# One sum of squares for both query tiles of a turn, taken after the second tile's projection

## The chip, the cores and the metric

The kernel runs on one core of one Trainium2 chip. The metric is the device time of one execution in microseconds; of several runs the median is compared. Lower is better. Engines are named as in the profile: PE (TensorE), ACT (ScalarE), DVE (VectorE), POOL (GpSimd), SP (SyncE, which issues the DMAs). PSUM is the memory that PE writes and that ACT and DVE read; POOL does not touch it here.

## What is computed

One layer of a hybrid decoder, for a prompt of 2048 tokens and 8 single-token samples, all in fp32. What matters for this change is the query path:

```python
h = _rmsnorm(x, norm_g) * (1.0 + scale) + shift
z = h @ w_in                                    # 1024 -> 6656 columns: q, k, v, gates, ...
q = _rmsnorm(q.reshape(B, T, N_HEADS, HEAD_DIM), q_g)     # 16 heads of 64
k = _rmsnorm(k.reshape(B, T, KV_HEADS, HEAD_DIM), k_g)    # 4 heads of 64
logits = einsum('bnqkgd,bnskd->bnkgqs', qb, kb) * ATT_SCALE + rel_bias   # banded, window 128
p = softmax over [logits, sink]
o = einsum('bnkgqs,bnskd->bnqkgd', p, vb)
ya = o * silu(ga)
```

Each query head is divided by the root of the mean of its 64 squares before the scores. The rest of the layer (a recurrent branch, gates, merge and output projection) is not touched.

## The kernel before

**Halves and turns.** The prompt is done in two halves (s = 0 and 1) of 1024 tokens, eight tiles of 128 tokens each. Each half has a key/value phase, then the attention phase (`phase_attn`), then a long planned stage of large matmuls. The attention phase is a software pipeline of N + 2 = 18 turns of the loop over `i`. `seq` lists 16 steps (u, tp): u is one of four groups of four heads, tp one of four pairs of token tiles. A turn works on three steps at once:

- step i: project the queries of two token tiles (`gemm_a`, 24 matmuls of 128x256 for each tile, both into one PSUM tile `ps_[i]`), square them on ACT and sum each head's 64 squares on DVE (`stage_a1`), turn the sums into reciprocal norms on POOL (`rstd_of`: one multiply-add, then a power of -0.5), and scale the queries on DVE (`stage_a2`);
- step i-1: transpose the scaled queries (`stage_b1`: PE, then ACT and DVE split them in a high and a low part), scores (`stage_b2`, PE), band, bias and row minimum on DVE and exponentials on ACT (`stage_b3`, once for each of the two tiles). The exponential's tile `lt` has a 129th column with the sink, which POOL copies there (`stage_b0`);
- step i-2: reciprocal of the row sums (DVE) and multiplication with it (POOL) (`stage_b4`), transposes of the probabilities (`stage_c1`: PE, then ACT copies them out and DVE multiplies with the causal mask `mcT`), the product with the values (`stage_c2`, PE) and the evacuation (`stage_c3`: on DVE where u is 0, on ACT otherwise).

**Order.** Inside the loop `pinned[0]` is set, so every engine's queue holds its instructions in the order in which the loop's code calls them, but for small moves of the scheduler; waits between engines are semaphores that the framework places by tile. A tile that PE, ACT and DVE share in PSUM is passed from one to the next. On PE a turn is: first tile's 24 projection matmuls, 4 transposes of `stage_b1`, second tile's 24 matmuls, 8 transposes of `stage_c1` (four for each tile, waiting for POOL's product), scores, values, next turn.

**Weights.** In some turns `weights` splits raw weights in two parts (a CAST on ACT, a subtraction on DVE); two such splits stand near the start of a turn.

**Buffers.** `M` tiles hold small statistics, `H` tiles come from a pool of six, `Tt` takes the oldest idle one of 35 numbered buffers ("B" in the profile) and `free` puts it back at the end of the list. In the profile nearly all instructions carry line L60, a helper; they are told apart by their tiles: `H<-pg` on ACT is the square, `M<-H` on DVE the sum of squares, `M<-M,mhalf` on POOL the power, `B<-pg,M` on DVE the scaling, `B<-B,M` 128x129 on ACT the exponential, `B<-B,M` 128x512 on POOL the product of `stage_b4`, `pt<-ident,B` on PE the transposes, `B<-skn` on POOL the copy of the sinks, `maskf` and `mcT` the masks, and `S<-pt` on ACT the evacuation `stage_c3`.

Of the kernel before, what the change touches and what calls it, by code (L numbers as in the profile page):

```python
# [15 lines left out]
AF = mybir.ActivationFunctionType  # L16
ALU = mybir.AluOpType
AX = mybir.AxisListType
# [8 lines left out]
HD = 64  # L27
# [14 lines left out]
def tile_hybrid_step(ctx: ExitStack, tc: tile.TileContext, x_prompt, x_sample, cache_k, cache_v, state_conv,  # L42
# [24 lines left out]
    V, A, G_, T_, ld = (Pinned(e) for e in (nc.vector, nc.scalar, nc.gpsimd, nc.tensor, nc.sync))  # L67
# [14 lines left out]
    def nm(s):  # L82
        cnt[0] += 1
        return f"{s}_{cnt[0]}"
# [14 lines left out]
    S, Tt = (r.get for r in rings)  # L99

    def free(*ts):
        for t in ts:
            r = rings[id(t) in rings[1].held]
            r.idle.append(r.held.pop(id(t))[1])

    def H(shape, dt=F32):
        return hp.tile([P] + shape, dt, tag="H", name=nm("H"))

    def M(shape, dt=F32):

        return mp.tile([P] + shape, dt, tag="M", name=nm("M"))

    def PG():
        return pg.tile([P, 512], F32, tag="g", name=nm("pg"))
# [4 lines left out]
    def PT():  # L119
        return pt.tile([P, 512], F32, tag="t", name=nm("pt"))  # L120
# [30 lines left out]
    def drop(ws):  # L151

        seen = set()
        for w in ws:
            if id(w[2][0]) not in seen:
                seen.add(id(w[2][0]))
                free(*w[2])
# [33 lines left out]
    def gemm_a(ps, wu, xs, c0, h):  # L191

        o = ps[:, h * 256:(h + 1) * 256]
        for k in range(KT):
            wh, wl, _ = wu[k]
            xh, xl = col(xs, k, c0, P)
            T_.matmul(o, xh, wh, start=(h == 0 and k == 0), stop=False, skip_group_check=True)
            T_.matmul(o, xh, wl, start=False, stop=False, skip_group_check=True)
            T_.matmul(o, xl, wh, start=False, stop=(k == KT - 1), skip_group_check=True)
# [40 lines left out]
    def rstd_of(dst, ss, n, inv):  # L240
        G_.tensor_scalar(dst, ss, inv, EPS, op0=ALU.mult, op1=ALU.add)
        G_.tensor_tensor(dst, dst, mhalf[0:dst.shape[0], 0:n], op=ALU.pow)
# [9 lines left out]
    ps = PT()  # L252
# [305 lines left out]
    def phase_attn(s, hT, sa, kT, vt, chunks, line):  # L558

        ya, mbs, kcs = {}, {}, {}  # L560

        def stage_a1(ps, ss, t):
            sq = H([256])
            A.activation(sq, ps[:, t * 256:(t + 1) * 256], AF.Square)
            o = ss[:, 4 * t:4 * t + 4]
            V.tensor_reduce(o, sq.rearrange("p (h d) -> p h d", d=HD), op=ALU.add, axis=AX.X)
            rstd_of(o, o, 4, 1.0 / HD)

        def stage_a2(ps, ss):
            qn = Tt([2, 2, 2, HD])  # L570
# [73 lines left out]
        def stage_b4(lt, sm):  # L644
            V.reciprocal(sm, sm)
            G_.tensor_tensor(lt[:, :, 0:P], lt[:, :, 0:P], sm.unsqueeze(2).broadcast_to([P, 4, P]), op=ALU.mult)
            return lt
# [69 lines left out]
        N = len(seq)  # L717
# [14 lines left out]
        def ga_half(n):  # L732


            f, c, h = GA[n // nt], n % nt // 2, n % 2
            c0, w = chunks[c]
            if h == 0:
                gps[0] = PG()
                if c == 0 and f < KT:
                    ya[f] = S([1024])  # L740
            ps = gps[0]
            for k in range(4 * h, 4 * h + 4):
                wh, wl, _ = wga[f][k]
                xh, xl = col(hT, k, c0, w)
                T_.matmul(ps[:, :w], wh, xh, start=(k == 0), stop=False)
                T_.matmul(ps[:, :w], wh, xl, start=False, stop=False)
                T_.matmul(ps[:, :w], wl, xh, start=False, stop=(k == KT - 1))
            if h == 0:
                return None

            def evac_ma():
                t = Tt([512])
                A.activation(t[:, :w], ps[:, :w], AF.Tanh, scale=0.5)
                st.dma_start(tmad[s, f - KT, :, c0:c0 + w], t)
                free(t)

            def evac():
                sg = ya[f]
                t = Tt([512])
                A.activation(t[:, :w], ps[:, :w], AF.Tanh, scale=0.5)  # L760
                V.scalar_tensor_tensor(sg[:, c0:c0 + w], t[:, :w], 1.0, ps[:, :w], op0=ALU.add, op1=ALU.mult)
                free(t)

            if c == len(chunks) - 1:
                drop(wga.pop(f))
            return evac if f < KT else evac_ma
# [46 lines left out]
        ps_, ss_, qn_, qk_, c_, sm_, lt_ = {}, {}, {}, {}, {}, {}, {}  # L813
        for i in range(N + 2):
            gsm_ready = len(gsm)

            def fill(n):
                nonlocal hdone
                while hdone < n:
                    evac = ga_half(hdone)  # L820
                    if evac:
                        evac()
                    hdone += 1

            def slot(n):
                if N - 3 <= i <= N:
                    line.emit(4 * (i - N - 1) + n)

            if 2 <= i:
                lt_[i - 2] = [stage_b4(*sm_[i - 2][0])]  # L830
            weights(2 * i, 0)
            if 2 <= i:
                lt_[i - 2].append(stage_b4(*sm_.pop(i - 2)[1]))
            if 1 <= i <= N:
                ub, tb = seq[i - 1]
                if tb == 0 and ub % 2 == 0:
                    mbs[ub // 2] = S([8, P])
                    ld.dma_start(mbs[ub // 2], Md[:, ub // 2 * 8:ub // 2 * 8 + 8])
            slot(0)
            if i < N:  # L840
                u, tp = seq[i]
                ps_[i], ss_[i] = PG(), M([8])
                gemm_a(ps_[i], wqs[u], hT, 2 * tp * P, 0)
                stage_a1(ps_[i], ss_[i], 0)
            elif i == N:
                fill(nh - 3)
            else:
                line.emit(0)
            if 1 <= i <= N:
                qk_[i - 1] = stage_b1(ub, tb, qn_.pop(i - 1))  # L850
            weights(2 * i, 1)
            slot(1)
            if i < N:
                if s == 1 and tp == 1:
                    next(smp[u])
                if pend:
                    next(pend.pop(0))
                gemm_a(ps_[i], wqs[u], hT, (2 * tp + 1) * P, 1)
                if pend:
                    next(pend.pop(0))  # L860
                if tp == 3:
                    drop(wqs.pop(u))
                if s == 1 and tp == 1:
                    next(smp[u])
                stage_a1(ps_[i], ss_[i], 1)
            elif i == N:
                fill(nh - 2)
            else:
                line.emit(1)
            weights(2 * i + 1, 0)  # L870
            if 2 <= i:
                t2 = seq[i - 2][1]
                c_[i - 2] = [stage_c1(2 * t2 + t, lt) for t, lt in enumerate(lt_.pop(i - 2))]
                c_[i - 2] = [fn() for fn in c_[i - 2]]
            slot(2)
            if i == N + 1:
                line.emit(2)
            if 1 <= i <= N:
                lps = stage_b2(ub, tb, *qk_.pop(i - 1))
                lts = [stage_b0(ub) for _ in range(2)]  # L880
            if 2 <= i:
                u2, t2 = seq[i - 2]
                po = stage_c2(u2, c_.pop(i - 2))
                if u2 == 3:
                    free(vt[1][t2])
            if 1 <= i <= N:
                sm_[i - 1] = [stage_b3(ub, 2 * tb, lps[0], lts[0])]
            if i < N:
                qn_[i] = stage_a2(ps_.pop(i), ss_.pop(i))
            if 2 <= i and u2 > 0:  # L890
                stage_c3(u2, t2, po)
            if 1 <= i <= N:
                sm_[i - 1].append(stage_b3(ub, 2 * tb + 1, lps[1], lts[1]))
                if ub % 2 and tb == 3:
                    free(mbs.pop(ub // 2), *kT[ub // 2])
            fill(want[i] if i < N else nh)
            if 2 <= i and u2 == 0:
                stage_c3(u2, t2, po)
            if 2 <= i and t2 == 3:
                for f in (2 * u2, 2 * u2 + 1):  # L900
                    st.dma_start(yad[s, f], ya[f])
                    free(ya.pop(f))
            weights(2 * i + 1, 1)
            if s == 1 and i < N and tp > 0:
                next(smp[u])
            if gsm and gsm_ready:
                next(gsm.pop(0))
            slot(3)
# [1108 lines left out]
    for f in range(KT):  # L2017
# [19 lines left out]
        for tt in range(4):  # L2037
            c = slice(tt * P, (tt + 1) * P)
            for j in range(2):
                wh, wl, _ = wkv[f // 4][j][f % 4]  # L2040
                o = kvp[tt][:, j * 256:(j + 1) * 256]
# [51 lines left out]
    ps = PT()  # L2093
# [51 lines left out]
```

## Time and profile before

| what | value |
|---|---|
| median of 3 runs | 1988.05 us (1987.31 to 1990.62) |
| profiled execution | 1991.77 us, span 1990.1 us, clock 0.995 |
| busy: PE / PE weight loads / DVE / ACT / POOL | 1930.7 / 1571.9 / 1375.0 / 988.4 / 409.4 us |
| attention phase, steady turns | first half about 152 to 316 us of the span, second about 1092 to 1266 us |
| a steady turn | 11 to 13 us |

A row of the timeline gives start, length, engine, operation with the tiles it writes and reads, and, in brackets, how long the engine had stood idle before it and for whom. PE is 97% busy, so the share of busy time says little of what one change is worth; the few idle moments of PE and what ends them say more.

### The profile page before, as it was taken

To read this page: it belongs to the slowest core of one execution; us is meant where nothing else is said; L and a number is where in the kernel's file an instruction comes from. 1 tells how busy PE (TensorE), PEld (TensorE's weight loads), DVE (VectorE), ACT (ScalarE), POOL (GpSimd) and SP (SyncE) were. 2 spreads that over 40 slices of the span, in tenths; PEclk is the share of its full clock that TensorE was granted. 3 is DMA by queue.
4 is the path that set the end of the run, shared out by engine and by line. 5 is a ranking of instruction groups with operands and counts; after the bars stand their busy time and mean duration, and the time that the engine had idled before them with its cause. 6 is when DMAs were issued, how large, how long until landed. Compare 5 with 4: busy or idle time off the path is not lost. (4 is left out here: it accounts for less than half of the span.)

```text
span 1990.1 us, 32504 instructions
## 1 busy us (share of the span) xinstructions
PE 1930.7 (97%) x11504; PEld 1571.9 (79%) x11504; DVE 1375.0 (69%) x2894; ACT 988.4 (50%) x2199; POOL 409.4 (21%) x540
## 2 busy tenths in 40 slices
PE   6899999999999999999999999999999999999999
PEld 4788887778888878887898888777887877777777
DVE  3447777766878885578744766677677879754965
ACT  4335555435665766514423555543465757542221
POOL 4113443000201112152012344310011111111600
PEclk9999999999999999999999999999999999999999
DMA  9520214552433457986622121445233334458673
GB/s 304 178 75 12 86 49 148 151 183 87 150 98 113 143 180 226 321 296 191 224 60 57 36 62 49 143 130 153 78 118 100 127 102 164 141 174 291 219 230 111
DMA packets 307688, 286.62 MB, mean 144 GB/s; under 512 B 57073, under 2 KB 224229, under 8 KB 307486
## 3 DMA queue, kind: packets, MB, share of 16 engines
q1 hardware_dynamic: 307398, 282.41, 45.3%
q8 instruction: 90, 1.47, 0.3%
q0 software_dynamic: 128, 2.15, 0.3%
q14 instruction: 72, 0.59, 0.1%
HBM read 200.69 MB, written 85.93 MB: 144 GB/s over the span
## 5 line engine op out<-in xcount | busy, mean ns | idle before, releaser
L60 PE MATMUL pg<-S,B 128*128 128x512 f32 (+1 forms) x4224 | 1003.8, 392 | 4.2 <-DVE B L60 3.8
L60 PEld LDWEIGHTS pg<-S,B 128*128 128x128 f32 (+1 forms) x4224 | 773.5, 188 | 189.5 <-issue 11.9
L60 DVE TENSOR_TENSOR B<-B,B 128x512 fp32r<-128x512 f32 (+1 forms) x732 | 537.8, 757 | 157.7 <-ACT B L60 147.9
L60 PE MATMUL pq<-S,B 128*128 128x512 f32 (+2 forms) x1920 | 411.0, 378 | 5.9 <-DVE B L60 5.7
L60 PEld LDWEIGHTS pq<-S,B 128*128 128x128 f32 (+1 forms) x1920 | 316.3, 187 | 84.1 <-DVE B L60 9.7
L60 POOL TENSOR_TENSOR B<-B,B 128x512 f32<-128x512 f32 x128 | 191.3, 1511 | 926.3 <-DVE B L60 518.3
L60 ACT CAST B<-B 128x512 fp32r<-128x512 f32 x468 | 280.3, 617 | 111.2 <-DVE B L60 72.1
L60 PE MATMUL pg<-B,S 128*128 128x256 f32 x1872 | 249.0, 289 | 17.6 <-ACT H L60 12.8
L60 PEld LDWEIGHTS pg<-B,S 128*128 128x128 f32 x1872 | 231.9, 192 | 36.6 <-ACT H L60 19.8
L60 ACT CAST S<-B 128x512 fp32r<-128x512 f32 x184 | 108.8, 620 | 95.8 <-DVE B L60 40.3
L60 DVE TENSOR_TENSOR S<-B,S 128x512 fp32r<-128x512 f32 x184 | 143.2, 808 | 14.8 <-ACT S L60 14.6
L60 ACT ACTIVATE B<-B 128x512 f32<-128x512 f32 (+1 forms) x150 | 93.1, 630 | 116.4 <-DVE B L60 108.7
L60 ACT ACTIVATE B<-B,M 128x129 f32<-128x129 f32 x260 | 102.6, 396 | 72.1 <-DVE M L60 53.4
L60 POOL TENSOR_TENSOR B<-B,M 128x512 f32<-128x512 f32 x64 | 70.4, 1121 | 170.4 <-DVE M L60 170.4
L60 DVE SCALAR_TENSOR_TENSOR B<-B,pg 128x512 f32<-128x512 f32 x78 | 53.1, 682 | 74.8 <-PE pg L60 67.0
L60 POOL TENSOR_TENSOR M<-M,mhalf 128x4 f32<-128x4 f32 (+3 forms) x102 | 96.3, 944 | 8.5
L60 DVE TENSOR_TENSOR B<-pq,B 128x512 f32<-128x512 f32 x96 | 65.9, 686 | 44.1 <-PE pq L60 37.9
L60 ACT COPY B<-pg 128x512 f32<-128x512 f32 x80 | 46.9, 586 | 90.1 <-PE pg L60 81.7
L60 DVE TENSOR_REDUCE M<-H 128x4 f32<-128x256 f32 (+1 forms) x85 | 35.1, 414 | 80.3 <-ACT H L60 79.0
L60 ACT COPY H<-pt 128x256 f32<-128x256 f32 (+1 forms) x47 | 15.6, 333 | 150.1 <-PE pt L60 150.1
L60 DVE SCALAR_TENSOR_TENSOR B<-B,VT,B 128x512 f32<-128x512 f32 x96 | 81.1, 845 | 2.3
L60 DVE SCALAR_TENSOR_TENSOR B<-B,B 128x512 f32<-128x512 f32 x106 | 72.0, 684 | 0.4 <-ACT B L60 0.2
(201 smaller groups left out, 1711.5 us busy)
## 6 DMA issues: line engine op xcount, KB each, us to landing
B<-in_w_in_dram SPq DMA_DIRECT2D x144, 256.0 KB
B<-in_w_in_dram SPq DMA_DIRECT2D x128, 128.0 KB
B<-yad SPq DMA_DIRECT2D x56, 256.0 KB
B<-hd SPq DMA_DIRECT2D x48, 256.0 KB
B<-in_w_out_dram SPq DMA_DIRECT2D x48, 256.0 KB
S<-in_w_ada_dram SPq DMA_DIRECT2D x32, 256.0 KB
S<-in_x_prompt_dram SPq DMA_DIRECT2D x16, 512.0 KB
hd<-B SPq DMA_DIRECT2D x32, 256.0 KB
```

The lines of the kernel that those rows point to most:

```text
L60: ins = fn(*args, **kw)
```

## The change

The square and the sum of squares are no longer taken tile by tile. Before, each tile's 256 columns were squared right after that tile's 24 matmuls, summed by head into four columns, and turned into four reciprocal norms. Now ACT squares all 512 columns of the PSUM tile once, after the second tile's matmuls (`stage_a1`, into a B buffer instead of an H tile), and DVE sums all eight heads at once and POOL takes all eight reciprocal norms at once in a new `stage_a3`, which is called later: after `stage_c1`'s mask multiplications and ahead of the scores.

```diff
-        def stage_a1(ps, ss, t):
-            sq = H([256])
-            A.activation(sq, ps[:, t * 256:(t + 1) * 256], AF.Square)
-            o = ss[:, 4 * t:4 * t + 4]
-            V.tensor_reduce(o, sq.rearrange("p (h d) -> p h d", d=HD), op=ALU.add, axis=AX.X)
-            rstd_of(o, o, 4, 1.0 / HD)
+        def stage_a1(ps):
+            sq = Tt([512])
+            A.activation(sq, ps, AF.Square)
+            return sq
+
+        def stage_a3(sq):
+            ss = M([8])
+            V.tensor_reduce(ss, sq.rearrange("p (h d) -> p h d", d=HD), op=ALU.add, axis=AX.X)
+            free(sq)
+            rstd_of(ss, ss, 8, 1.0 / HD)
+            return ss
...
                 gemm_a(ps_[i], wqs[u], hT, 2 * tp * P, 0)
-                stage_a1(ps_[i], ss_[i], 0)
...
                 gemm_a(ps_[i], wqs[u], hT, (2 * tp + 1) * P, 1)
...
-                stage_a1(ps_[i], ss_[i], 1)
+                sq = stage_a1(ps_[i])
...
                 c_[i - 2] = [fn() for fn in c_[i - 2]]
+            if i < N:
+                ss_[i] = stage_a3(sq)
             slot(2)
```

What this does to the queues is shown for one turn of the first half (i = 7; the buffer numbers differ between the kernels).

DVE, from a weight split and the two reciprocals of `stage_b4` to the first mask of the scores, before:

```order
L60 TENSOR_TENSOR B_2583<-B_1962,B_2582 128x512
L60 RECIPROCAL M_2558<-M_2558 128x4
L60 RECIPROCAL M_2577<-M_2577 128x4
L60 TENSOR_REDUCE M_2591<-H_2616 128x4
L60 SCALAR_TENSOR_TENSOR B_2627<-pt_2621,qg_944,B_2626 128x512
L60 TENSOR_TENSOR B_2631<-B_1965,B_2630 128x512
L60 TENSOR_REDUCE M_2591<-H_2664 128x4
L60 TENSOR_TENSOR B_2679<-pt_2669,mcT_90 128x512
L60 TENSOR_TENSOR B_2683<-pt_2674,mcT_90 128x512
L60 COPY_PREDICATED pq_2687<-maskf_88,pq_2687 128x2x128
```

and with the change:

```order
L60 TENSOR_TENSOR B_2548<-B_1941,B_2547 128x512
L60 RECIPROCAL M_2523<-M_2523 128x4
L60 RECIPROCAL M_2542<-M_2542 128x4
L60 SCALAR_TENSOR_TENSOR B_2586<-pt_2580,qg_944,B_2585 128x512
L60 TENSOR_TENSOR B_2590<-B_1944,B_2589 128x512
L60 TENSOR_TENSOR B_2635<-pt_2625,mcT_90 128x512
L60 TENSOR_TENSOR B_2639<-pt_2630,mcT_90 128x512
L60 TENSOR_REDUCE M_2643<-B_2623 128x8
L60 COPY_PREDICATED pq_2647<-maskf_88,pq_2647 128x2x128
```

Two sums of four heads, one before the query split and one ahead of the mask multiplications, have become one sum of eight heads between the mask multiplications (`mcT`) and the scores' first mask (`maskf`).

PE in the same turn, with the semaphores waited for: the four transposes of `stage_b1` between the two tiles' projections, before:

```order
L60 MATMUL pt_2621<-ident_81,B_2563 128x128 [waits DVE_49,PE_49]
L60 MATMUL pt_2621<-ident_81,B_2563 128x128
L60 MATMUL pt_2621<-ident_81,B_2563 128x128 [waits DVE_49]
L60 MATMUL pt_2621<-ident_81,B_2563 128x128
L60 MATMUL pg_2590<-B_1711,S_337 128x256 [waits Activation_49]
```

and with the change:

```order
L60 MATMUL pt_2580<-ident_81,B_2528 128x128 [waits DVE_49,PE_49]
L60 MATMUL pt_2580<-ident_81,B_2528 128x128
L60 MATMUL pt_2580<-ident_81,B_2528 128x128 [waits DVE_49]
L60 MATMUL pt_2580<-ident_81,B_2528 128x128
L60 MATMUL pg_2555<-B_1701,S_337 128x256
```

PE's order is the same, but the second tile's first matmul no longer waits for ACT.

POOL in the same turn, from the products of `stage_b4` to the two copies of the sinks, before:

```order
L60 TENSOR_TENSOR B_2540<-B_2540,M_2558 128x4x128
L60 TENSOR_TENSOR B_2542<-B_2542,M_2577 128x4x128
L60 TENSOR_SCALAR M_2591<-M_2591 128x4
L60 TENSOR_TENSOR M_2591<-M_2591,mhalf_94 128x4
L60 TENSOR_SCALAR M_2591<-M_2591 128x4
L60 TENSOR_TENSOR M_2591<-M_2591,mhalf_94 128x4
L60 COPY B_2715<-skn_950 128x4
L60 COPY B_2717<-skn_950 128x4
```

and with the change:

```order
L60 TENSOR_TENSOR B_2505<-B_2505,M_2523 128x4x128
L60 TENSOR_TENSOR B_2507<-B_2507,M_2542 128x4x128
L60 TENSOR_SCALAR M_2643<-M_2643 128x8
L60 TENSOR_TENSOR M_2643<-M_2643,mhalf_94 128x8
L60 COPY B_2675<-skn_950 128x4
L60 COPY B_2677<-skn_950 128x4
```

Two pairs of four columns have become one pair of eight, still ahead of the copies of the sinks. On ACT the square between the exponentials and the query split is gone and the one behind the query split is 512 wide instead of 256. SP's queue holds the same DMAs in the same order.

More of the change, by code (lines that the diff above doesn't have):

```diff
@@ L841, in phase_attn @@
                 u, tp = seq[i]
-                ps_[i], ss_[i] = PG(), M([8])
+                ps_[i] = PG()
                 gemm_a(ps_[i], wqs[u], hT, 2 * tp * P, 0)
-                stage_a1(ps_[i], ss_[i], 0)
             elif i == N:
```

## Prediction

> **What bounds the kernel now.** I read the page's busy shares first, then the two attention stretches, then what PE waits for in them, then single turns.
>
> ```profile
> PE 1930.7 (97%) x11504; PEld 1571.9 (79%) x11504; DVE 1375.0 (69%) x2894; ACT 988.4 (50%) x2199; POOL 409.4 (21%) x540
> ...
> 152.00:316.00 164.00, 157.49 (x1393) 137.02 (x1393) 118.43 (x427) 92.56 (x324) 67.97 (x111) 1.00 0.17 53
> 1092.00:1266.00 174.00, 167.31 (x1496) 144.69 (x1495) 123.15 (x442) 100.70 (x349) 72.95 (x117) 1.00 0.16 50
> ```
>
> PE fills 97% of the span, and in the two stretches of attention turns (columns: stretch, length, then busy time of PE, weight loads, DVE, ACT, POOL) it idles 6.5 of 164 and 6.7 of 174 us. No change there can win more than these 13 us. Who is waited for, in the first and in the second stretch:
>
> ```profile
> PE pg L60 <- ACT H L60: 6.1, 12, 1.1
> ...
> PE pg L60 <- ACT H L60: 3.8, 5, 1.0
> PE pt L60 <- POOL B L60: 1.2, 4, 0.3
> ```
>
> In 17 turns, 9.9 us in all, the second tile's projection (`pg`) waits for ACT's square of the first tile (`H`); that is the wait that the change takes away. [...]
>
> **Where these waits stand.** Two kinds of turns. In the plain ones they are small, and the product on POOL that `stage_c1`'s transposes need is ready long before:
>
> ```profile
> 188.20 3.10 PE L60 MATMUL pg<-B,S 128*128 128x256 f32 x24 [0.19 <-ACT H L60]
> 191.14 1.04 PE L60 MATMUL pt<-ident,B 128*128 128x128 f32 x8
> ...
> 188.07 2.04 POOL L60 TENSOR_TENSOR B<-B,M 128x512 f32<-128x512 f32 x2 [5.39 <-DVE M L60]
> ...
> 233.07 2.04 POOL L60 TENSOR_TENSOR B<-B,M 128x512 f32<-128x512 f32 x2 [4.72 <-DVE M L60]
> ...
> 236.81 1.04 PE L60 MATMUL pt<-ident,B 128*128 128x128 f32 x8
> ```
>
> The second four transposes start 0.43 after the first, at 191.57, and POOL was done at 190.11: 1.5 us to spare; at 237.24 against 235.11 it is 2.1. In the turns that begin with a weight split the wait is large, nine in all, first and last:
>
> ```profile
> 200.03 3.10 PE L60 MATMUL pg<-B,S 128*128 128x256 f32 x24 [0.93 <-ACT H L60]
> ...
> 1237.90 3.10 PE L60 MATMUL pg<-B,S 128*128 128x256 f32 x24 [0.52 <-ACT H L60]
> ```
>
> Four are in the first half (0.93, 1.04, 0.93, 1.07) and five in the second (1.03, 0.63, 1.03, 0.60, 0.52): 3.97 and 3.81 us, so the eight small ones make 2.1. One turn of this kind followed through the engines, from one set of `stage_c1`'s transposes (202.97) to the next (214.52):
>
> ```profile
> 202.97 1.03 PE L60 MATMUL pt<-ident,B 128*128 128x128 f32 x8
> ...
> 204.10 0.59 ACT L60 COPY B<-pt 128x512 f32<-128x512 f32 x1 [0.54 <-PE pt L60]
> ...
> 203.92 1.49 DVE L60 TENSOR_TENSOR B<-pt,mcT 128x512 f32<-128x512 f32 x2
> 205.33 0.42 DVE L60 COPY_PREDICATED pq<-maskf,pq 128x256 f32<-128x256 int32 x1
> ...
> 203.23 0.19 POOL L60 TENSOR_SCALAR M<-M 128x4 f32<-128x4 f32 x1
> 203.50 1.01 POOL L60 TENSOR_TENSOR M<-M,mhalf 128x4 f32<-128x4 f32 x1
> ...
> 204.87 1.01 POOL L60 TENSOR_TENSOR M<-M,mhalf 128x4 f32<-128x4 f32 x1
> 205.83 0.32 POOL L60 COPY B<-skn 128x4 f32<-128x4 f32 x2
> ...
> 206.23 0.40 ACT L60 ACTIVATE B<-B,M 128x129 f32<-128x129 f32 x1 [1.55 <-POOL B L60]
> ...
> 207.97 0.62 ACT L60 COPY S<-pt 128x256 f32<-128x256 f32 x2
> 208.93 0.41 ACT L60 ACTIVATE B<-B,M 128x129 f32<-128x129 f32 x1 [0.34 <-DVE M L60]
> ...
> 210.26 0.39 ACT L60 ACTIVATE B<-B,M 128x129 f32<-128x129 f32 x1
> ...
> 210.65 0.60 ACT L60 CAST B<-B 128x512 fp32r<-128x512 f32 x1
> ...
> 211.28 0.69 DVE L60 TENSOR_TENSOR B<-B,B 128x512 fp32r<-128x512 f32 x1 [1.18 <-ACT B L60]
> 211.89 0.23 DVE L60 RECIPROCAL M<-M 128x4 f32<-128x4 f32 x2
> ...
> 212.21 2.49 POOL L60 TENSOR_TENSOR B<-B,M 128x512 f32<-128x512 f32 x2 [6.05 <-DVE M L60]
> ...
> 214.52 1.04 PE L60 MATMUL pt<-ident,B 128*128 128x128 f32 x8
> ```
>
> This is a loop without a hole: transposes, ACT's copy, DVE's mask multiplications, the scores' masks and minima, eight exponentials, the CAST, the subtraction that waits for it, the reciprocals, POOL's product (ends 214.70), the second four transposes (214.95). PE had waited 1.04 us for the square in between, and still only 0.2 us were left at the end, a semaphore's 0.05 taken off. In the second half nothing is left:
>
> ```profile
> 1157.01 1.24 PE L60 MATMUL pt<-ident,B 128*128 128x128 f32 x8
> ...
> 1155.05 2.49 POOL L60 TENSOR_TENSOR B<-B,M 128x512 f32<-128x512 f32 x2 [6.22 <-DVE M L60]
> ```
>
> POOL ends at 1157.54 and the eight transposes take 1.24 instead of 1.04 us, because the last four wait for it. So in nine turns the loop through DVE, ACT and POOL sets the pace, and the wait for the square is idle time inside a wait that comes anyway.
>
> **The change part by part.** Prices (mean ns of one stand behind the busy time):
>
> ```profile
> L60 POOL TENSOR_TENSOR M<-M,mhalf 128x4 f32<-128x4 f32 x80 | 81.4, 1017 | 6.7
> L60 POOL TENSOR_TENSOR M<-M,mhalf 128x1 f32<-128x1 f32 x16 | 9.4, 589 | 1.3
> L60 DVE TENSOR_REDUCE M<-H 128x4 f32<-128x256 f32 x80 | 33.1, 414 | 78.8 <-ACT H L60 77.6
> L60 DVE TENSOR_REDUCE xrS<-pt 128x8 f32<-128x32 f32 x32 | 5.2, 184 | 14.1 <-PE pt L60 14.1
> L60 ACT ACTIVATE B<-pg 128x512 f32<-128x512 f32 x44 | 26.1, 593 | 47.0 <-PE pg L60 47.0
> L60 ACT ACTIVATE H<-pg 128x256 f32<-128x256 f32 x71 | 26.9, 379 | 85.3 <-PE pg L60 85.1
> ```
>
> *Removed: the wait of the second projection.* Worth the eight small waits, 2.1 us, where PE sets the pace; in the nine large ones worth only the slack that PE then has to wait out: 0.2 us in each of the four in the first half, nothing in the five others. Late next there is POOL's product.
>
> *The square.* One of 593 ns for two of 379: 0.17 us of ACT saved in each of 32 turns, off the path. The one that is left starts at the same moment as the second did before (the projection's end) and is done in the 0.9 us until ACT's first copy (203.17 to 204.10 here); cost 0. Where ACT copies both tiles, the copy starts 0.5 us after the square; a 512-wide ACT instruction is followed by the next after 0.51 (the CAST at 210.65, its successor at 211.16): cost 0.0.
>
> *The sum of squares, moved.* From 32 to 256 elements the sum grows by 1.03 ns an element, so 512 take about 414 + 263 = 677 ns (estimate), against 828 for two. DVE saves 0.15 us a turn, 4.8 us in all, and none of it counts: the first sum stood behind the reciprocals and the second ahead of a wait, both outside the loop. [...] But the new sum stands between the mask multiplications and the scores' mask, inside the loop. An instruction starts about 0.08 before the one ahead ends, so the scores begin 0.60 us later, in every turn.
>
> *The power on POOL, and what is queued behind it.* Nothing in the trace takes eight columns. From one to four it grows by 143 ns a column, so eight take 589 + 7 x 143 = 1.59 us; from below it is 1.02 (as four), from above 2.03 (two of four). I take 1.59, the line through both rows. Behind it on POOL stand the copies of the sinks, and for these the first exponential waits already now (206.23, 1.55 <-POOL). In the turn shown: the sum runs from 205.33 to 206.01, POOL's multiply-add starts 0.09 later and the power 0.27 after that, at 206.37, to 207.96; the copies start at 207.91 and the first exponential 0.40 later as now, at 208.31. Four of them at 0.40 and the two evacuation copies (0.62) bring the fifth to 210.53 and the eighth to 211.73; now it starts at 210.26. So the loop grows by 1.5 us. In the first head group the evacuation is on DVE, not on ACT, and the same count without the 0.62 gives the eighth 5.18 us after the scores' first mask (2.38 + 7 x 0.40), now 4.93: 0.25 and the 0.60 make 0.8. The scaling of the queries, which waits for the power, comes at 208.0 instead of 207.93 (DVE's own time): nothing.
>
> *Registers and queues.* PE and SP keep their order. The square sits in a B buffer for part of a turn; loads of weights into these buffers are issued turns ahead of their split, and that distance is the cover; without it a late load would cost what it is late. Cost 0.
>
> **The sum.** Plain turns: -2.1. They can take the longer loop: 1.5 us to spare against 0.8 in the first head group, 2.1 against 1.5 later, less the 0.2 to 0.4 that PE comes earlier. Turns with a split, first half: 0.8 - 0.2 = 0.6 once and 1.5 - 0.2 = 1.3 three times, 4.5; second half: 0.8 once and 1.5 four times, 6.8. In all -2.1 + 4.5 + 6.8 = +9.2 us. After the attention turns PE works without holes again, so the shift reaches the end. The profiled execution (1991.77, of which 1990.1 are the span) lies 3.7 above the median; it would become 2001.0. On the median of 1988.05 the forecast is 1997.3, 0.46% slower.
>
> Ends from the power: at 1.02 the two lengthenings are 0.60 and 0.95, and the sum is -2.1 + 0.4 + 2.25 + 0.6 + 3.8 = +5.0 (1993.0). At 2.03 they are 1.2 and 2.0: -2.1 + 1.0 + 5.4 + 1.2 + 8.0 = +13.5, and the plain turns begin to wait as well, some 1.5 more: 2003.
>
> **Rivals.** *Faster, by the waits removed.* If the loop had room, all 9.9 us would come: 1978.2. For it: 17 waits that vanish for certain. Against it: the product ends 0.25 us or less before the transposes that need it in all nine split turns. Even if the loop did not grow at all, the gain would be 2.1 + 0.8 = 2.9 (1985.2). It decides if the loop grows by less than 0.1 us in the second half, that is, if the sum is hidden. Chance 0.06.
>
> *No change.* The sum's 0.6 counts, but the exponentials are not held up, because the copies of the sinks or the power prove shorter than the line says: -2.1 + 4 x 0.4 + 5 x 0.6 = +2.5, 1990.6. Against it: the exponential does wait for POOL now. Chance 0.14.
>
> *More.* The power takes twice that of four columns, or DVE, in order, carries the delay into the planned stage behind the first half, which starts with waits for DVE: 2003 and above. Chance 0.13. The forecast, from 1993 to 2003, keeps 0.67.
>
> The range is 1990.5 to 2003.0. Less than 0.2% (4 us) is about what a measurement of this kernel cannot tell from no change; faster by more 0.06, within it 0.14, slower 0.80.
>
> **What would show it.** After: no wait of `pg` for an ACT square between `stage_b1`'s transposes and the second projection; in its place waits of `pt` for POOL's `B` in the split turns, about 1.5 us each and more, some 14 us in all; a power of eight columns near 1.59 us; the first exponential about 2.4 us after the scores' first mask, where it is 0.9 now. I am wrong if PE's waits for POOL stay near 1 us (then the loop has room), or if the power is not the length assumed.

## The result and the profile after

| | median, us | ratio to the kernel before, 95% interval |
|---|---|---|
| before | 1986.13 (1983.63 to 1990.62) | |
| with the change | 1993.78 (1990.18 to 1995.49) | 1.0032 [1.0022, 1.0041] |
| with the change, a second series (before: 1987.66) | 1992.35 | 1.0024 [1.0014, 1.0034] |

By the ratios the change makes the kernel 5 to 6 us slower (the medians differ by 7.7 and 4.7). The forecast was +9.2 us, 1997.3; the time lies inside its range, and the sign is as forecast. The sum, however, was put together partly from wrong sizes and lacks two terms, as is shown below.

The two profiled executions are equally long (spans 1990.1 and 1990.4). The second four transposes of the first steady turn (i = 2) begin at 153.21 before and at 147.20 after, and from these to the same ones of the last turn of the second half (1283.48 and 1283.53) it is 1130.27 against 1136.33 us, **+6.06**; what follows is equal (706.6 and 706.8). The 6.0 us ahead of the first steady turn have two parts, for PE's order is the same in both kernels and each matmul can be found again. Up to 112 us of the span of before, ahead of the attention phase's first wait, it is 1.7 us; a second profile of the change is 6.1 us ahead there, so this is scatter of the start. The other 4.3 us, from there to the first steady turn, are the same in both profiles of the change, and they count in the table below.

PE is nearly as busy as before, in the page's first line of after:

```profile
PE 1927.6 (97%) x11504; PEld 1572.2 (79%) x11504; DVE 1373.8 (69%) x2862; ACT 975.1 (49%) x2167; POOL 388.7 (20%) x476
```

The other three all work less (DVE 1.2, ACT 13.3, POOL 20.7 us), and the kernel is still slower. The waits of PE say why. Over 80 to 1300 us, which takes in both attention phases, before and then after (columns: total us, times, longest):

```profile
PE pg L60 <- ACT H L60: 12.8, 19, 1.8
PE pt L60 <- ACT S L60: 2.7, 2, 1.4
PE pt L60 <- POOL B L60: 1.4, 5, 0.3
```

```profile
PE pt L60 <- POOL B L60: 16.1, 17, 2.8
PE pt L60 <- ACT S L60: 4.6, 2, 3.4
```

The wait for the square is gone, in all 19 places (two of them, at 116.76 and 1055.68, lie in turn 0 of the halves, outside the windows that the prediction read). In its place PE waits for POOL's product. The groups show what became slow ahead of that product; the exponentials of before, then three groups of after:

```profile
L60 ACT ACTIVATE B<-B,M 128x129 f32<-128x129 f32 x260 | 102.6, 396 | 72.1 <-DVE M L60 53.4 <-POOL B L60 12.9 <-DVE pq L60 2.0
```

```profile
L60 ACT ACTIVATE B<-B,M 128x129 f32<-128x129 f32 x260 | 101.7, 395 | 110.2 <-POOL B L60 105.8 <-DVE M L60 4.2
L60 POOL TENSOR_TENSOR M<-M,mhalf 128x8 f32<-128x8 f32 x32 | 52.4, 1638 | 2.7
L60 DVE TENSOR_REDUCE M<-B 128x8 f32<-128x512 f32 x32 | 21.7, 677 | 5.5 <-ACT B L60 5.5
```

ACT now idles 105.8 us ahead of its exponentials for POOL's `B`, the tile with the copied sinks, where it was 12.9. One power of eight columns takes 1638 ns, one sum 677.

The turn of the prediction, as it runs now, from one set of `stage_c1`'s transposes (196.71) to the next (209.24):

```profile
196.71 0.66 PE L60 MATMUL pt<-ident,B 128*128 128x128 f32 x4 [0.79 <-POOL B L60]
...
198.02 0.69 DVE L60 TENSOR_TENSOR B<-pt,mcT 128x512 f32<-128x512 f32 x1 [1.38 <-ACT B L60]
198.63 0.68 DVE L60 TENSOR_REDUCE M<-B 128x8 f32<-128x512 f32 x1
...
199.22 0.42 DVE L60 COPY_PREDICATED pq<-maskf,pq 128x256 f32<-128x256 int32 x1
199.39 0.20 POOL L60 TENSOR_SCALAR M<-M 128x8 f32<-128x8 f32 x1 [2.74 <-DVE M L60]
...
199.68 1.64 POOL L60 TENSOR_TENSOR M<-M,mhalf 128x8 f32<-128x8 f32 x1
...
201.26 0.32 POOL L60 COPY B<-skn 128x4 f32<-128x4 f32 x2
...
201.49 0.41 ACT L60 ACTIVATE B<-B,M 128x129 f32<-128x129 f32 x1 [3.50 <-POOL B L60]
...
203.05 0.62 ACT L60 COPY S<-pt 128x256 f32<-128x256 f32 x2
...
204.74 0.40 ACT L60 ACTIVATE B<-B,M 128x129 f32<-128x129 f32 x1
205.13 0.61 ACT L60 CAST B<-B 128x512 fp32r<-128x512 f32 x1
...
205.77 0.69 DVE L60 TENSOR_TENSOR B<-B,B 128x512 fp32r<-128x512 f32 x1 [1.66 <-ACT B L60]
206.38 0.23 DVE L60 RECIPROCAL M<-M 128x4 f32<-128x4 f32 x2
...
206.70 2.48 POOL L60 TENSOR_TENSOR B<-B,M 128x512 f32<-128x512 f32 x2 [5.12 <-DVE M L60]
...
209.24 0.44 PE L60 MATMUL pt<-ident,B 128*128 128x128 f32 x2 [0.79 <-POOL B L60]
```

The chain is the forecast one: the sum (198.63) pushes the scores' first mask to 199.22; the power (199.68 to 201.32) keeps the copies of the sinks back; the first exponential starts 2.27 us after the mask, the eighth at 204.74, 5.52 after it (4.94 in the same turn before). POOL's product ends at 209.18, and PE, which has waited for it, goes on at 209.24. The turn takes 12.53 us instead of 11.56.

All turns, after minus before, in us ("again" is a second profile of the change). A turn i is counted from the second four transposes of turn i-1 to those of turn i; the first turns of each half run from the same matmul in both kernels (at 112.0 and 1050.0 before) to the second four transposes of turn i = 2:

| part | forecast | after | again |
|---|---|---|---|
| first turns, first half | 0 | -4.27 | -4.28 |
| split turns, first half (4) | +4.5 | +3.29 | +3.25 |
| split turns, second half (5) | +6.8 | +5.39 | +5.81 |
| other turns to i = 15, both halves (17) | -2.1 | -5.23 | -3.74 |
| last two turns, first half | 0 | +0.54 | +0.57 |
| last two turns, second half | 0 | +4.66 | +4.75 |
| stage between the halves | 0 | -0.69 | -1.44 |
| first turns, second half | 0 | -1.88 | -1.88 |
| sum | +9.2 | +1.8 | +3.0 |

The sums are the 6.06 us of above, and 7.3 in the second profile, less the 4.3 of the first turns. These are single executions, and the sums stay below the 5 to 6 us of the medians. What fills the difference is open; that the clock has a part in it is argued in the next section.

### The profile page after: what moved, and what is told of

Same layout as the page of the kernel before. It is cut to its first block, busy times and chain, and to the rows that moved or that the text cites. A ratio compares the mean times of both kernels' runs of the same rounds, so it can differ in the third digit from the quotient of the medians.

```text
span 1990.4 us, 32374 instructions
## 1 busy us (share of the span) xinstructions
PE 1927.6 (97%) x11504; PEld 1572.2 (79%) x11504; DVE 1373.8 (69%) x2862; ACT 975.1 (49%) x2167; POOL 388.7 (20%) x476
## 5 line engine op out<-in xcount | busy, mean ns | idle before, releaser
L60 PEld LDWEIGHTS pg<-B,S 128*128 128x128 f32 x1872 | 230.9, 191 | 16.1 <-issue 9.8
L60 ACT ACTIVATE B<-B,M 128x129 f32<-128x129 f32 x260 | 101.7, 395 | 110.2 <-POOL B L60 105.8
L60 POOL TENSOR_TENSOR M<-M,mhalf 128x8 f32<-128x8 f32 (+4 forms) x70 | 83.9, 1199 | 5.8
L60 ACT ACTIVATE B<-pg 128x512 f32<-128x512 f32 x76 | 45.2, 595 | 80.9 <-PE pg L60 80.8
L60 DVE TENSOR_TENSOR B<-pt,mcT 128x512 f32<-128x512 f32 x64 | 42.2, 687 | 51.6 <-ACT B L60 49.2
```

Of the source, the lines that this page charges most:

```text
L60: ins = fn(*args, **kw)
```

## What was not forecast: one turn, and the clock

In turn i = 16 of the second half PE does a piece for the samples, `pt<-B,hsF`, whose PSUM buffer ACT's evacuation copies of `stage_c3` must first set free. These copies stand behind the exponentials that the power holds up. Before:

```profile
1258.27 0.62 ACT L60 COPY S<-pt 128x256 f32<-128x256 f32 x2
...
1258.94 0.65 PE L60 MATMUL pt<-B,hsF 128*32 128x128 f32 x16 [1.43 <-ACT S L60]
1259.51 3.07 PE L60 MATMUL pg<-S,B 128*128 128x512 f32 x12
```

After:

```profile
1255.60 0.62 ACT L60 COPY S<-pt 128x256 f32<-128x256 f32 x2
...
1256.27 1.08 PE L60 MATMUL pt<-B,hsF 128*32 128x128 f32 x16 [3.36 <-ACT S L60]
1257.27 5.33 PE L60 MATMUL pg<-S,B 128*128 128x512 f32 x12
```

The wait has grown from 1.43 to 3.36 us, and the same 12 matmuls take 5.33 instead of 3.07 us. The windows give the reason; the granted clock is the first number behind the five engines. After:

```profile
1188.00:1190.00 2.00, 2.00 (x17) 1.67 (x17) 1.23 (x3) 0.59 (x1) 0.00 (x0) 0.50 0.00 0
...
1254.00:1258.00 4.00, 1.74 (x18) 1.22 (x19) 3.00 (x15) 3.96 (x19) 1.16 (x3) 0.68 0.00 0
1258.00:1262.00 4.00, 4.00 (x11) 3.13 (x10) 1.34 (x1) 0.28 (x1) 1.06 (x2) 0.50 0.00 0
1262.00:1266.00 4.00, 4.00 (x22) 3.23 (x22) 1.37 (x2) 1.50 (x4) 0.00 (x0) 0.96 0.00 0
```

In the trace's clock record the half clock begins at 1255.5, inside the wait, and lasts 6.83 us, so PE runs at half speed for about six microseconds behind the wait; 1188 to 1190 lies behind a wait of 2.78 us. In the same stretch before, where the wait was 1.43 us, the clock stays at 1.00. The wait alone was worth 1.9 us; the slower matmuls, another 2.7, make the turn's 4.6.

The clock is a larger part of the loss than this one turn. Without the stage between the halves the table's parts make +2.5 and +4.5 us. Slow stretches in them are worth 1.6 us before (turn 0, below) and, with the change, 2.7 in turn 16 and 0.5 in i = 11 of the second half (13.32 us, where i = 7, at full clock, takes 12.85); the second profile has 0.5 more in i = 7 and 1.5 in i = 12 of the first half. Without them both profiles come to about +0.9. In the record of all executions the mean granted clock is 0.9960 and 0.9965 before (17 and 23 executions), 0.9928 and 0.9926 with the change (10 and 11) and 0.9972 with the sum called early (5). The change loses some 0.0035, which would be 7 us of 1990; by this estimate the clock can cost no more than that. How much of it stood on PE's path in the executions without a trace isn't shown.

## The experiments

All start from the kernel with the change; the first four ran beside before at 1989.41 us, the last three beside before at 1987.66.

**The sum called early.** The same merged instructions, with `stage_a3` right behind the square.

```diff
                 sq = stage_a1(ps_[i])
+                ss_[i] = stage_a3(sq)
...
-            if i < N:
-                ss_[i] = stage_a3(sq)
             slot(2)
```

> One square of both tiles as in the change, but the sum of eight heads and the power are called right behind the square, ahead of the mask multiplications. Loop theory (the change costs because the sum and the power lengthen the loop transposes - DVE - ACT - POOL - transposes in nine split turns): in the split turns the square is done before the transposes come, so the sum leaves the loop; the loop is as long as before (11.3 to 11.6 us in the first half's split turns, not 12.5), the plain turns keep their gain (about 4 us in the first half) and turn 0 of each half its own (about 3 us): 4 to 8 us faster than before, ratio 0.996 to 0.998. Rival (the wide square, or the B buffer that holds it, costs by itself): as slow as the change, 1.002 to 1.004.

Measured: 1976.76 us, ratio **0.994 [0.9928, 0.9951]**: 12.6 us under the kernel before and more than was expected; the rival is out. PE's waits for POOL over the same 80 to 1300 us:

```profile
PE pt L60 <- POOL B L60: 8.5, 12, 1.7
```

The eighth exponential comes 4.94 us after the scores' mask, as before. From the first steady turn to the last, the first half is 4.48 us shorter than before, the second 0.32, and the part between the halves 2.20. That makes 7.0 of the 12.6. The first turns of the first half are 4.2 us shorter, as with the change, and the tail 0.5, so that 11.8 are found. So merging and taking PE's wait away are a gain; what loses is the place of the call.

**The copies of the sinks ahead of the power.** The sum stays late; `rstd_of` is called after `stage_b0`, so that POOL copies the sinks first.

```diff
             V.tensor_reduce(ss, sq.rearrange("p (h d) -> p h d", d=HD), op=ALU.add, axis=AX.X)
             free(sq)
-            rstd_of(ss, ss, 8, 1.0 / HD)
             return ss
...
                 lts = [stage_b0(ub) for _ in range(2)]
+            if i < N:
+                rstd_of(ss_[i], ss_[i], 8, 1.0 / HD)
```

> The change, but the copies of the sinks stand ahead of the power in POOL's queue; the sum stays behind the mask multiplications. Loop theory with two terms: the first exponential comes 0.9 to 1.0 us after the scores' first mask instead of 2.3, the eighth 4.9 instead of 5.5; the loop keeps the sum's 0.6 us and loses the other 0.6 in nine turns, and the sample product near the end of the second half waits some 1.4 us for ACT instead of 3.4: 5 to 8 us faster than the change, ratio to before 0.999 to 1.001. Rival (the sum alone lengthens the loop): as the change, 1.003.

Measured: 1986.23 us, ratio 0.9987 [0.9977, 0.9997], just under the range that was expected.

```profile
PE pt L60 <- POOL B L60: 12.2, 14, 2.3
```

The first exponential is back at 0.91 to 0.99 us behind the mask, and the loop of the split turn i = 7, from its second four transposes to the end of POOL's next product, is 12.00 us long: 11.29 before, 12.48 with the change. So of the 1.19 that the change adds to this loop 0.71 is the late sum's and 0.48 the power's ahead of the copies. The sample product's wait is 2.2 us, not the expected 1.4, since the late sum alone delays the exponentials too; in this profile turn i = 16 of the second half still takes 15.18 us, where it is 12.90 before.

**Both.** The sum early and the power behind the copies (the two edits above together).

> Sum right behind the square, power behind the copies of the sinks. Loop theory: as the version with the early sum or up to 1 us faster, since the power no longer stands ahead of the copies: ratio 0.995 to 0.998. Rival (the wide square or its buffer costs): 1.002 or more.

Measured: 1980.57 us, ratio 0.9958 [0.9945, 0.997]. Its steady turns add up as those of the sum called early (174.59 and 190.50 us, there 174.64 and 190.50): with the sum early, the power's place makes nothing. The 3.8 us between the two medians lie outside these turns, and their cause stays open; the intervals overlap. In the two profiles the difference lies in the start ahead of 112 us (3.5) and in the stage between the halves (2.3); the start scatters by 4.4 us between the two profiles of the change, too.

**The wait kept.** The change, but with two squares of 256 columns into one tile, the first right behind the first tile's matmuls, so that the second projection has to wait as before.

```diff
-        def stage_a1(ps):
-            sq = Tt([512])
-            A.activation(sq, ps, AF.Square)
-            return sq
+        def stage_a1(ps, sq, t):
+            A.activation(sq[:, t * 256:(t + 1) * 256], ps[:, t * 256:(t + 1) * 256], AF.Square)
```

> The change, but the square is again taken tile by tile (two squares of 256 into one buffer), so that the second projection waits for the first square as before; sum and power as in the change. Loop theory with gains in the plain turns: the plain turns lose the 0.4 us each that the change won there, and turn 0 its 2 to 3 us: 5 to 8 us slower than the change, ratio to before 1.006 to 1.008. Rival (the waits taken away brought nothing): as the change, 1.003.

Measured: 2011.78 us, ratio 1.0124 [1.0109, 1.0138], 18 to 19 us over the change, where 5 to 8 were expected.

```profile
PE pg L60 <- ACT B L60: 33.7, 23, 2.2
```

```profile
206.37 0.39 ACT L60 ACTIVATE B<-B,M 128x129 f32<-128x129 f32 x1
...
207.27 0.38 ACT L60 ACTIVATE B<-pg 128x256 f32<-128x256 f32 x1
```

```profile
207.70 3.12 PE L60 MATMUL pg<-B,S 128*128 128x256 f32 x24 [2.17 <-ACT B L60]
```

The waits are not the 12.8 us of before but 33.7: the first square stands on ACT behind the eighth exponential (206.37) and a CAST, and as the exponentials have become late, so has the square, and PE waits 2.17 us for it. The two parts of the change don't add up: with late exponentials the kept wait, with its second square, costs 18 to 19 us (2011.78 against 1992 to 1994), not the 10 to 13 that the profile of before shows.

**The last turn alone.** The sum and power early in turn i = 15 only.

```diff
                 sq = stage_a1(ps_[i])
+                if i == N - 1:
+                    ss_[i] = stage_a3(sq)
...
-            if i < N:
+            if i < N - 1:
                 ss_[i] = stage_a3(sq)
```

> The change, except that in the last turn with queries (i = 15, in both halves) the sum and the power are called right behind the square, ahead of the mask multiplications. Theory (the late exponentials of that turn hold ACT's evacuation copies, and PE's sample product waits for these): in the second half the wait of `pt<-B,hsF` for ACT's `S` falls from 3.36 to some 1.5 us, the half-clock stretch behind it goes too, the turn loses the 4.6 us that it had gained, and the first half's loses 0.3: some 4 to 5 us under the change, ratio to the kernel before near 1.001 (0.9995 to 1.002). Rival (that wait belongs to the place of the run's DMAs and would have come anyway): wait of 3 us and more stays, ratio as the change, 1.003.

Measured: 1989.98 us, ratio 1.0012 [1.0002, 1.0021].

```profile
1254.88 0.64 PE L60 MATMUL pt<-B,hsF 128*32 128x128 f32 x16 [1.61 <-ACT S L60]
1255.45 3.04 PE L60 MATMUL pg<-S,B 128*128 128x512 f32 x12
```

The wait is 1.61 us, the matmuls run at full clock, and turn i = 16 takes 13.10 us, where the change has 17.51 and 17.59. So the last turn's loss is that of the exponentials one turn earlier, and not of this execution's transfers. The medians of this series differ by 2.4 us only, not by the turn's 4.5; in this profile two other turns (i = 8 and 12 of the first half) are 1.5 us longer each than in the first profile of the change, with the clock down behind two waits of some 1.0 and 0.8 us, with four transposes (0.66 us) between them. Behind the first pair (1.03 at 204.17 and 0.79 at 205.61):

```profile
206.00:208.00 2.00, 2.00 (x21) 1.83 (x21) 1.30 (x3) 0.58 (x1) 0.00 (x0) 0.62 0.00 0
```

**The change again,** unchanged.

> The change once more, for a second profile with another start-up. Theory: ratio 1.002 to 1.004; the same turns are longer by the same amounts within 0.2 us (split turns 0.9 to 1.0 in the first half, 1.1 to 1.6 in the second), the wait of the sample product in the last turn is above 3 us again, and what differs is where a long PE wait is followed by matmuls at half the clock. Rival (the turn lengths of one profile are chance): they scatter by half a microsecond and more.

Measured: 1992.35 us, 1.0024 [1.0014, 1.0034]. The wait in turn 16 is 3.35 us again. Of the 30 turn lengths 28 lie within 0.1 us of the first profile's. The others are i = 7 of the second half (+0.46, granted clock 0.58 from 1133 to 1137) and i = 12 of the first (+1.52), with a granted clock of 0.79 and 0.72 in two windows from 250 to 257; waits of 1.01 to 1.04 and 0.79 us stand ahead of it in both profiles, but in the first the clock stays at 1.00.

**The sum twice.** The same sum done a second time in its new place.

```diff
             V.tensor_reduce(ss, sq.rearrange("p (h d) -> p h d", d=HD), op=ALU.add, axis=AX.X)
+            V.tensor_reduce(ss, sq.rearrange("p (h d) -> p h d", d=HD), op=ALU.add, axis=AX.X)
             free(sq)
```

> The change with the sum of the eight heads done twice in its new place (the second overwrites the first with the same values). Theory (between the mask multiplications and the scores' first mask everything lies in the loop, one for one, in the nine split turns, and plain turns still have slack): the loop of a split turn grows by another 0.60 us, 5.4 us in nine turns, the last turn's wait by 0.6, 1.2 at the half clock: some 6 us over the change, ratio 1.006 (1.005 to 1.008). Rival 1 (DVE's own time sets the pace of all turns): 32 times 0.6, 19 us over the change, 1.013. Rival 2 (the power alone holds the exponentials, and the sum is hidden): as the change, 1.003.

Measured: 2003.35 us, ratio 1.0082 [1.0066, 1.0098], 11.0 us over the change in the same series instead of the 6 expected; the direction is right, and both rivals are out. Two sums back to back:

```profile
172.66 1.39 DVE L60 TENSOR_REDUCE M<-B 128x8 f32<-128x512 f32 x2
```

The second adds 0.71 us, not 0.60, and the loop of a split turn grows by it, from 12.46 (the second profile of the change) to 13.18 us (i = 7 of the first half). What was missed is the plain turns: with the change the product was ready 0.28 us ahead of its transposes in turns i = 4 and 5 and 0.43 in i = 15 (first half), so another 0.7 us turns them into waiting turns as well, by 0.3 to 0.5 us each. In the second half i = 4, 8, 12 and 15 grow by 0.5 to 1.0 us although the product is ready there in time: in i = 4 PE waits for DVE's `M` (1.08 us, 0.36 with the change), in 8 and 12 for ACT's `S` (0.33 and 0.32, no such wait with the change), and in 15 the clock is down (0.57 from 1243 to 1247). The wait of the sample product grows to 4.08 us.

## Why the prediction was right, and where it was off

- *The loop sets the pace in the split turns*: shown. The early sum takes the loop's growth out and wins; doing the sum twice lengthens it by the sum. With that the rival *faster, by the waits removed* is out, and so is *no change* in its mechanism, for the exponentials are held up (2.27 us behind the mask). Of *more*, the power is not twice as long, and the stage between the halves is not longer.
- *The price of the power*, 1.59 us by a line through one and four columns: 1.64. *The sum*, 677 ns estimated: 677. *The square at no cost*: no new wait for it on PE.
- *The loop's growth, 1.5 us* (0.8 in the first head group): 1.19 in the turn shown, 0.76 in a turn of the first group. The exponentials were 0.3 us early against the count: the first came 2.27 instead of 2.38 us after the mask, and the two evacuation copies kept the queue for 0.52 (203.05 to 203.57), where 0.62 was put in. This mis-sizing is the 2.6 us too much in the split turns (2.2 in the second profile, where a slow stretch stands in one more of them).
- *The small waits, 2.1 us*: too small. The other turns gained 5.2 us (3.7 in the second profile, 5.3 without its slow stretch in i = 12). The idle time that a row books was less than the stall. One such turn, before and then after:

```profile
187.41 0.60 PE L60 MATMUL pt<-ident,B 128*128 128x128 f32 x4
```

```profile
180.70 0.60 PE L60 MATMUL pt<-ident,B 128*128 128x128 f32 x4
181.06 1.19 PE L60 MATMUL pg<-B,S 128*128 128x256 f32 x8
```

From the transposes to the projection it was 0.79 us (188.20 less 187.41) with 0.19 booked as idle, and it is 0.36 now: 0.43 gained. Without a wait the projection starts 0.24 us before the row of the transposes ends (181.30). So the idle time of PE in the two stretches, 6.5 and 6.7 us, was no upper bound of what could be won there.
- *The first turns at nothing*: the term that was most off. The waits of turn 0 (1.84 and 1.05 us) were not counted, since the windows began later; both halves together gain 6.2 us in their first turns. Turn 0 of the first half, before and then after:

```profile
116.76 4.64 PE L60 MATMUL pg<-B,S 128*128 128x256 f32 x24 [1.84 <-ACT H L60]
```

```profile
112.92 3.07 PE L60 MATMUL pg<-B,S 128*128 128x256 f32 x24
```

The wait is gone, worth 2.1 us between starts, and so is a stretch at half clock, 1.6. That second part need not be the change's: the run that keeps the wait has no such stretch either (its granted clock is 1.00 from 80 to 150 us).
- *The last turns at nothing*: wrong, +4.7 in the second half. The prediction followed the delayed exponentials only to POOL's product, not to the copies behind them and PE's wait for these, and did not know what the clock makes of a long wait.
- *Waits for POOL of some 14 us*: 16.1.

The prediction's own terms, put right, still make a loss: 3.29 + 5.39 - 5.23 = +3.4 us in the first profile, and about +2.9 in both when the slow stretches are left out, so the forecast sign comes from its mechanism. That the time fell inside its range is in part luck: the first turns (-6.2) and the last (+5.2), both put at nothing, nearly cancel, and the slow stretches of PE's clock, which the prediction did not have, add to the loss.

## What to carry to other kernels

Two small operations merged into one were cheaper here (a square of 595 ns for two of 379, a sum of 677 for two of 414, a power of 1638 for two of 1017), but the merged one is as late as its later input: ask what stands behind it in its engine's queue, and call it where that engine would wait anyway. Here the same instructions cost 5 to 6 us in one place and gain 12.6 in another, a few lines of code ahead. When PE waits, follow the other engines once around the loop before the wait is counted as a gain, and count the turns at the loop's start and end by themselves.

## What the chip did that was not expected

The granted clock fell to 0.50 behind waits of 2.78 and 3.36 us, as the windows above show, and 12 matmuls of 512 columns then took 5.33 instead of 3.07 us. It had fallen in the kernel before too, behind the wait of 1.84 us in turn 0:

```profile
117.00:121.00 4.00, 4.00 (x23) 4.00 (x23) 1.17 (x4) 0.37 (x1) 1.20 (x2) 0.58 0.07 30
```

It is no matter of the wait's length alone: with the change a wait of 1.78 us (at 1135.92) is followed by full speed (a granted clock of 1.00 from 1136 to 1140), in the second profile the same wait (at 1132.27) by a slow stretch (0.58 from 1133 to 1137); where the wait was kept, one of 2.17 us (at 207.70) is followed by full speed (24 matmuls in 3.12 us); and in the last-turn experiment the clock fell to 0.62 behind two short waits close together (1.03 and 0.79 us). The clock records of the first profiles, before and with the change, know full and half clock only; the slow stretches in them last 3.41 or 6.83 us, but for the one at the end of each (3.91 and 3.09). What decides whether a wait brings one isn't shown, and no experiment filled the wait with other matmuls; that the clock falls because of the wait is read from the order of rows alone.
